# A decoder trunk on one core: some low parts of the weights are formed on GpSimd instead of VectorE

## The chip, the core and the metric

The kernel runs on one core of a Trainium2 chip. The core has a matrix engine, TensorE (PE), and three engines for elementwise work: VectorE (DVE), ScalarE (ACT) and GpSimd (POOL). SyncE (SP) issues most of the DMAs. Each engine works through its own queue strictly in order and waits on semaphores for results of the others. The metric is the device time of one execution in microseconds; the median of several runs is compared. A profile is one execution that the hardware profiler recorded.

## What is computed

Two layers of a decoder trunk, batch 1, 512 tokens, model width 1024, float32. Cut to what matters here:

```python
D_MODEL, SEQ, DEPTH, D_IN = 1024, 512, 2, 3488

def hybrid_layer(x, ...):
    h = rmsnorm(x, norm_g)
    p = h @ w_in
    (cq, ckv, kr, g_a, c_h, c_b, c_c, g_b, sg_u, sg_v, g_c, mq, mk, mv, g_d) = jnp.split(p, offs, axis=-1)
    o_a = causal attention on low-rank q and kv, with a rotary key
    o_b = c_b * short_conv(c_c * c_h, conv_w)
    o_c = spatial_gate(sg_u, sg_v, sg_ln_g, sg_ln_b, sg_w, sg_b)
    o_d = block-sparse attention on mq, mk, mv
    y = jnp.concatenate([o_a * silu(g_a), o_b * silu(g_b), o_c * silu(g_c), o_d * silu(g_d)], axis=-1)
    return y @ w_out

def reference(x, ...):
    for l in range(DEPTH):
        x = x + hybrid_layer(x, ...)
    return x
```

The lines for `o_a` and `o_d` are put in words here. The two large products are `h @ w_in` and `y @ w_out`.

## The kernel before

**Three matmuls for one.** A float32 operand is split in a high part in the form fp32r, and a low part, the rest, also fp32r. A product is three matmuls, high by high, high by low and low by high (`mm3`, L282). Weights and activations alike are split: the high part is a copy to fp32r, mostly on ACT, and the low part a subtraction, `lo = raw - hi`, on DVE.

**Weight units.** The weights come in units of at most 128 x 1024 numbers (`Unit`, named `ga0_0`, `b211_1` and so on: the name, and the layer behind the last underscore; in the profile's tile names the numbers are left out, so `wlo_b` is the low part of any of the units b110 to b221). All units stand in one list, `order`, in the order in which PE uses them, and `u.idx` is a unit's place there. `load_units` (L405) brings each by a DMA on SP's queue into a raw buffer; `split_units` (L439) makes it into `whi` and `wlo`, and does so in two halves: a half is 512 columns (416 for the units named c). A unit's raw buffer is free when both low halves are done, and the next load waits for it. There are two raw buffers and a few borrowed ones, and six pairs of `whi` and `wlo`.

**The planner.** The program is written out by a planner in Python, before anything runs. Each stretch of work is a generator; `Order` (L74) keeps a clock `o.now` that PE's matmuls advance by an assumed cost, and a clock for each other engine: `o.clk["A"]` for ACT, `"V"` for DVE, `"G"` for POOL, `"D"` for DMA. `Chain._emit` (L173) writes an instruction into its engine's queue when its operands are due by these clocks, and adds the assumed cost to the engine's clock. So the order in every queue is fixed by assumed costs, while the chip follows the semaphores. `at[0]` is the place of the unit that PE has reached, and a unit is "wanted" when it is less than `AHEAD` = 4 places on. `split_units` starts a half when ACT and DVE have nothing left by their clocks, or when the unit is wanted. `low_half` (L474) then holds the low half back while DVE is more than `VSLACK` = 300 ns behind and the unit is more than `URGENT` = 2 places ahead.

**What runs on POOL.** The rotary tables in the first 40 us; then a few powers that give reciprocal square roots (`pow_rstd`, L713: the tiles `ms`, `bmv`, `rs_q`, `rs_k`, `rs_mq`, `rs_mk`, `xss`), some fills (`kl0d`, `kl1d`), and accumulating DMAs (`t_sums`, L356). These last belong to the large products that are computed with seven products instead of eight: units named t1 to t4 (for `w_out`) and p1 to p4 (for a part of `w_in` in layer 1) are sums of blocks of the weights. They are built in DRAM by a copy on SP's queue and an adding DMA on POOL's queue, which waits for the copy; later copies wait for earlier sums.

**Stages that the prediction speaks of.** In each layer the products with activations come first, attention runs among them, and the last stage (`seven`, L1823) is `y @ w_out`: the products b11, t3, b21, t4, t2, t1 and b22. Each takes two units and 24 matmuls, 12 for each of two output tiles, so a unit is used up every 2.7 us there, twice as fast as elsewhere. A unit's two halves belong to two blocks of rows of the weights, and the second half is read three matmuls after the first or later; b211 is the second unit of b21, t41 that of t4. PE writes the results to PSUM tiles named oz, ox, oy and ot. DVE forms sums of activations there (`ys`, `u`), their low parts (`yTl`, `suml`) and the residual sums (`xr`).

Of the kernel before, what the change touches and what calls it, by code (L numbers as in the profile page):

```python
# [11 lines left out]
F32 = mybir.dt.float32  # L12
# [3 lines left out]
ALU = mybir.AluOpType  # L16
# [14 lines left out]

NRAW, NW, NT2 = 2, 6, 11
WSLACK = 0.0
AHEAD, URGENT, VSLACK = 4, 2, 300.0
NWARM, FILL, FILLEND = 6, 0.9, 15000.0
MIXT, MIXLAG, ROWT, COLT = 42000.0, 2000.0, 36000.0, 17500.0
KSPLIT, HMEAN = 6, 0.0
# [1 line left out]
LOPRIO = -5  # L39
# [119 lines left out]
def free_size(ap):  # L159
    n = 1  # L160
    for d in ap.shape[1:]:
        n *= d
    return n


class Chain:
# [24 lines left out]

    def pool(self, f, *a, **k):
        return self._emit("G", 290 + 2.0 * free_size(a[0]), f, a, k)

    def pow(self, f, *a, **k):
        return self._emit("G", 400 + 165 * free_size(a[0]), f, a, k)
# [24 lines left out]
def hybrid_trunk(ctx: ExitStack, tc: tile.TileContext, x, positions, norm_g, w_c, w_f, w_t, w_o, mla_q_norm_g,  # L221
# [3 lines left out]
    V, A, G, PE = nc.vector, nc.scalar, nc.gpsimd, nc.tensor  # L225
# [16 lines left out]
    o = Order()  # L242
# [196 lines left out]
    def split_units(i0, i1):  # L439
        for u in order[i0:i1]:  # L440
            ch = Chain(o)
            if u.name != "c0_0":
                yield from ch.wait(u.loaded)
            u.hi, u.lo = yield from u.slots.get(ch, u.name)
            n = u.a * u.b
            gain = {"uq": 2 * int(u.name[-1]), "ukv": 4 + int(u.name[-1])}.get(u.name[:-2])
            if gain is not None:
                yield from ch.wait(pc_ev)
            for i in range(2):
                if u.name == "c0_0":  # L450
                    yield from ch.wait(u.landed[i])
                while ch.t > o.now + SLACK:
                    yield ch.t - SLACK
                while not u.wanted and max(o.clk["A"], o.clk["V"]) > o.now + WSLACK:
                    yield o.now + 100.0
                sl = slice(i * n // 2, (i + 1) * n // 2)
                c2 = Chain(o, max(o.now, ch.t))
                hi, lo, raw = u.hi[:, sl], u.lo[:, sl], u.raw[:, sl]
                g = None
                if gain is not None:  # L460
                    c = gain + (i if u.a == 2 else 0)
                    g = pcol[:, c:c + 1]
                if o.clk["V"] + 600.0 < o.clk["A"] and u.idx > 3 or u.idx == 0 and i == 0:
                    if g is None:
                        yield from c2.dve_fast(V.tensor_copy, hi, raw)
                    else:
                        yield from c2.dve(V.tensor_scalar, hi, raw, g, None, op0=ALU.mult)
                else:
                    yield from c2.act(A.activation, hi, raw, AF.Copy, scale=1.0 if g is None else g)
                o.set(u.high[i], c2.t)  # L470
                o.spawn(low_half(u, i, c2, lo, raw, hi, g), None, LOPRIO if u.idx < 4 else 5)
                ch.t = max(ch.t, c2.t - LAT)

    def low_half(u, i, ch, lo, raw, hi, g):  # L474
        while o.clk["V"] > o.now + VSLACK and u.idx > at[0] + URGENT:
            yield o.now + 100.0
        ch.t = max(ch.t, o.now)
        if g is None:
            yield from ch.dve(V.tensor_tensor, lo, raw, hi.bitcast(F32), op=ALU.subtract)
        else:  # L480
            yield from ch.dve(V.scalar_tensor_tensor, lo, in0=raw, scalar=g, in1=hi.bitcast(F32),
                              op0=ALU.mult, op1=ALU.subtract)
        o.set(u.half[i], ch.t)
        if u.half[1 - i].t is not None:
            ch.t = max(ch.t, u.half[1 - i].t)
            u.raw_slots.put(ch)
            o.set(u.ready, ch.t)

# [9 lines left out]
    at = [0]  # L498
# [1507 lines left out]
    def start():  # L2006
# [32 lines left out]
        for u in order[:10]:  # L2039
            u.wanted = True  # L2040
        o.spawn(load_units(), None, 4)
        o.spawn(split_units(0, 4), None, LOPRIO)
        o.spawn(split_units(4, len(order)), None, 5)
        o.spawn(rope_tables(), 3700.0, 4)
        o.spawn(x_stats(), None, 5)
# [55 lines left out]
```

## Time and profile before

| what | value |
|---|---|
| median of 3 runs | 489.66 us (489.42 to 490.87) |
| the profiled execution's own time | 489.51 us |
| its span, first to last instruction | 487.8 us |
| granted TensorE clock, mean | 0.999 |
| TensorE busy | 480.9 us, 2432 matmuls |
| VectorE busy | 402.3 us, 897 instructions |
| ScalarE busy | 329.7 us, 912 instructions |
| GpSimd busy | 104.0 us, 172 instructions |
| DMA | 92.89 MB, mean 190 GB/s |

How to read the lines in this document. In a timeline or a chain a line begins with the start and the length in microseconds, then the engine, the line of the kernel, the operation, and the tiles `out<-in` with their shapes; a bracket at the end tells how long the engine sat idle before it and what ended that. Most instructions have L178, the line of the planner that emits them, and matmuls L208; so tiles tell them apart. In a group, `x32 | 20.8, 682` means 32 instructions, 20.8 us busy, 682 ns of one on average. In the waits, `A <- B: total, times, longest` means that engine and tile A waited for B. Instructions of an engine overlap a little, so a duration can be longer than the distance between two starts. The ends of matmuls are modelled; their starts are recorded.

### The profile page before, as it was taken

Reading aid. Unit: us, or ns where it says so; the run is one execution under the profiler, and the core shown is the slowest. Engines: PE = TensorE matmul, PEld = TensorE weight load, DVE = VectorE, ACT = ScalarE, POOL = GpSimd, SP = SyncE. Lnnn points to the kernel's source line nnn. Section 1 sums busy time; section 2 is a strip of 40 time slices with the busy share of each in tenths; the row PEclk is TensorE's granted clock in tenths of the full one; section 3 lists DMA queues with packets and bytes.
Section 4 is the critical chain, followed back from the end, with each engine's and each line's share of the span. In section 5 each row is a group of like instructions: output and inputs, shape, how many; then the busy total and the mean of one; then the engine's idle time right before and its main releaser. Section 6 shows DMA issues by size and latency. Waiting matters only on the chain.

```text
span 487.8 us, 7534 instructions
## 1 busy us (share of the span) xinstructions
PE 480.9 (99%) x2432; PEld 408.4 (84%) x2432; DVE 402.3 (82%) x897; ACT 329.7 (68%) x912; POOL 104.0 (21%) x172
## 2 busy tenths in 40 slices
PE   8999999999999999999999999999999999999997
PEld 8987888888878888888899988888888888888786
DVE  3687788769788897789898688979788998997993
ACT  6887857766447885447577788768675687666740
POOL 7864150710321020000031013520402200000000
PEclk9999999999999999999999999999999999999999
DMA  8433536997599688875663286786832744427762
GB/s 285 173 105 114 172 116 230 235 197 152 178 315 283 171 208 209 289 264 202 206 237 141 80 285 241 176 243 169 209 132 87 151 141 140 173 66 264 275 215 88
DMA packets 41904, 92.89 MB, mean 190 GB/s; under 512 B 7158, under 2 KB 23048, under 8 KB 41480
## 3 DMA queue, kind: packets, MB, share of 16 engines
q1 hardware_dynamic: 29168, 79.82, 47.1%
q0 software_dynamic: 12672, 12.58, 16.7%
q8 instruction: 19, 0.31, 0.3%
q14 instruction: 21, 0.17, 0.1%
q10 hardware_dynamic: 24, 0.01, 0.0%
HBM read 84.53 MB, written 33.03 MB: 241 GB/s over the span
## 4 chain that ended last, share of the span: by engine, by line
PE 96%; DVE 2%; ACT 0%; issue 0%; DVEq 0%; ACTq 0%
PE cq L208 8%; PE oy L208 6%; PE kv L208 6%; PE gd L208 5%; PE gb L208 5%; PE cb L208 5%; PE ch L208 5%; PE su L208 5%; PE gc L208 5%; PE cc L208 5%; PE ga L208 4%; PE sq L208 4%; PE oz L208 4%; PE py L208 3%; PE ox L208 3%; PE sa L208 3%
## 5 line engine op out<-in xcount | busy, mean ns | idle before, releaser
L178 ACT ACTIVATE pd<-pd,mnd 128x384 f32<-128x384 f32 (+3 forms) x48 | 25.4, 550 | 3.1 <-DVE mnd L178 2.8
L178 ACT ACTIVATE pha<-pTa 128x512 fp32r<-128x512 f32 (+3 forms) x32 | 13.9, 435 | 19.4 <-PE pTa L208 19.1
L178 ACT ACTIVATE pa<-pa,mna 128x384 f32<-128x384 f32 (+3 forms) x46 | 24.3, 550 | 2.4 <-DVE mna L178 2.3
L178 ACT ACTIVATE phd<-pTd 128x512 fp32r<-128x512 f32 (+3 forms) x32 | 13.9, 437 | 14.5 <-PE pTd L208 14.2
L372 POOL DMA_DIRECT2D t<-in_w_o_dram x16 | 17.2, 1323 | 22.3 <-DMA t<-t 22.3
L178 DVE TENSOR_TENSOR wlo_p<-raw_p,whi_p 128x512 fp32r<-128x512 f32 x28 | 19.1, 698 | 3.1 <-ACT whi_p L178 2.9
L178 DVE TENSOR_TENSOR pla<-pTa,pha 128x512 fp32r<-128x512 f32 (+3 forms) x32 | 15.3, 486 | 7.2 <-ACT pha L178 7.1
L208 PE MATMUL cq<-whi_c,hTh 128*128 128x416 f32 x64 | 20.5, 366 | 0.3 <-ACT hTh L178 0.3
L178 DVE TENSOR_TENSOR wlo_t<-raw_t,whi_t 128x512 fp32r<-128x512 f32 x32 | 20.8, 682 | 0.0
L208 PE MATMUL cq<-wlo_c,hTh 128*128 128x416 f32 x64 | 20.0, 359 | 0.0
L208 PE MATMUL cq<-whi_c,hTl 128*128 128x416 f32 x64 | 19.9, 356 | 0.0
L178 DVE CUSTOM_DVE_ANT_0 pa<-sa,maskb,rs_q 128x512 f32<-128x512 f32 (+3 forms) x32 | 16.5, 545 | 3.9 <-PE pTa L208 2.0
L178 ACT ACTIVATE whi_t<-raw_t 128x512 fp32r<-128x512 f32 x30 | 17.4, 618 | 1.6 <-DMA raw_t<-t 1.6
L178 DVE CUSTOM_DVE_ANT_0 pd<-sd,maskb,rs_mq 128x512 f32<-128x512 f32 (+3 forms) x32 | 16.9, 545 | 1.4 <-PE pTd L208 0.8
L178 POOL TENSOR_TENSOR rs_mk<-rs_mk,nhalf 128x16 f32<-128x16 f32 x2 | 6.2, 3083 | 51.1 <-DVE rs_mk L178 51.1
L178 DVE TENSOR_TENSOR pld<-pTd,phd 128x512 fp32r<-128x512 f32 (+3 forms) x32 | 15.2, 485 | 2.3 <-ACT phd L178 2.2
L178 POOL TENSOR_SCALAR xss<-xss 128x1 f32<-128x1 f32 x4 | 2.7, 670 | 66.1 <-ACT jk L178 61.8
L178 ACT ACTIVATE whi_b<-raw_b 128x512 fp32r<-128x512 f32 x23 | 14.0, 622 | 3.5 <-DMA raw_b<-in_w_o_dram 3.5
L178 ACT ACTIVATE whi_p<-raw_p 128x512 fp32r<-128x512 f32 x22 | 13.2, 624 | 4.4 <-DMA raw_p<-in_w_t_dram 4.4
L178 DVE TENSOR_TENSOR wlo_b<-raw_b,whi_b 128x512 fp32r<-128x512 f32 x24 | 16.0, 684 | 0.2
L208 PE MATMUL pTa<-ident,pa 128*128 128x128 f32 x80 | 14.0, 273 | 0.0
L208 PE MATMUL pTd<-ident,pd 128*128 128x128 f32 x80 | 13.9, 272 | 0.0
(470 smaller groups left out, 1853.3 us busy)
## 6 DMA issues: line engine op xcount, KB each, us to landing
t<-in_w_o_dram POOLq DMA_DIRECT2D x16, 512.0 KB, 8.1
raw_t<-t SPq DMA_DIRECT2D x16, 512.0 KB, 3.2
raw_b<-in_w_o_dram SPq DMA_DIRECT2D x12, 512.0 KB, 4.6
t<-in_w_o_dram SPq DMA_DIRECT2D x8, 512.0 KB, 4.4
p<-in_w_t_dram POOLq DMA_DIRECT2D x8, 512.0 KB, 13.1
t<-t SPq DMA_DIRECT2D x8, 512.0 KB, 6.8
raw_p<-p SPq DMA_DIRECT2D x8, 512.0 KB
ys<-ysc SPq DMA_DIRECT2D x14, 256.0 KB, 4.2
```

Source lines behind the costliest of these rows:

```text
L178: f(*a, **k)
L208: f(*a, **k)
L372: nc.gpsimd.dma_start(src(l, n, j), src(l, y, j), accum_op=ALU.add, max_dma_last_dim=1024)
```

## The change

The low part of a unit can now go to POOL. `split_units` forms the high part of a unit whole, in one instruction, when the unit is more than `WHOLE` = 2 places ahead of PE, has no gain and the clock is past `WHOLET` = 50,000 ns; otherwise in halves as before. `low_half` becomes `low_part`, which takes one half or both. While the unit is more than `URGENT` places ahead it asks, every 100 ns of the planner's clock: if POOL's queue is empty by its clock (and the unit has no gain and is more than `PLEAD` = 2 places ahead, past `WHOLET`), it emits the subtraction on POOL in pieces of `PCOLS` = 256 columns; if DVE is less than `VSLACK` behind, it goes to DVE in one instruction, 512 or 1024 columns wide; otherwise it asks again. The assumed cost of a piece on POOL is 200 + 1.65 ns a column.

```diff
-AHEAD, URGENT, VSLACK = 4, 2, 300.0
+AHEAD, URGENT, VSLACK, WHOLE, WHOLET = 4, 2, 300.0, 2, 50000.0
+PLEAD, GSLACK, PCOLS = 2, 0.0, 256
...
+    def pool2(self, f, *a, **k):
+        return self._emit("G", 200 + 1.65 * free_size(a[0]), f, a, k)
...
-            for i in range(2):
+            parts = [0, 1]
+            while parts:
+                i = parts[0]
...
-                sl = slice(i * n // 2, (i + 1) * n // 2)
+                ids = parts if i == 0 and gain is None and u.idx > at[0] + WHOLE and o.now > WHOLET else parts[:1]
+                parts = parts[len(ids):]
+                sl = slice(i * n // 2, (i + len(ids)) * n // 2)
...
-                o.set(u.high[i], c2.t)
-                o.spawn(low_half(u, i, c2, lo, raw, hi, g), None, LOPRIO if u.idx < 4 else 5)
+                for j in ids:
+                    o.set(u.high[j], c2.t)
+                o.spawn(low_part(u, ids, c2, lo, raw, hi, g), None, LOPRIO if u.idx < 4 else 5)
                 ch.t = max(ch.t, c2.t - LAT)
 
-    def low_half(u, i, ch, lo, raw, hi, g):
-        while o.clk["V"] > o.now + VSLACK and u.idx > at[0] + URGENT:
+    def low_part(u, ids, ch, lo, raw, hi, g):
+        while u.idx > at[0] + URGENT:
+            if g is None and u.idx > at[0] + PLEAD and o.clk["G"] <= o.now + GSLACK and o.now > WHOLET:
+                ch.t = max(ch.t, o.now)
+                for c in range(0, free_size(lo), PCOLS):
+                    z = slice(c, min(c + PCOLS, free_size(lo)))
+                    yield from ch.pool2(G.tensor_tensor, lo[:, z], raw[:, z], hi[:, z].bitcast(F32), op=ALU.subtract)
+                for j in ids:
+                    o.set(u.half[j], ch.t)
+                if None not in (u.half[0].t, u.half[1].t):
+                    ch.t = max(u.half[0].t, u.half[1].t)
+                    u.raw_slots.put(ch)
+                    o.set(u.ready, ch.t)
+                return
+            if o.clk["V"] <= o.now + VSLACK:
+                break
             yield o.now + 100.0
...
-        o.set(u.half[i], ch.t)
-        if u.half[1 - i].t is not None:
-            ch.t = max(ch.t, u.half[1 - i].t)
+        for j in ids:
+            o.set(u.half[j], ch.t)
+        if None not in (u.half[0].t, u.half[1].t):
+            ch.t = max(u.half[0].t, u.half[1].t)
             u.raw_slots.put(ch)
             o.set(u.ready, ch.t)
```

Because the planner's clocks change, it also writes the other instructions of the queues in another order from there on: PE has the same matmuls, with attention placed differently among the products.

## The prediction

> **What bounds the kernel now.** I read the page's totals first, then the waits of TensorE, then the chain of work that ended last.
>
> ```profile
> span 487.8 us, 7534 instructions
> PE 480.9 (99%) x2432; PEld 408.4 (84%) x2432; DVE 402.3 (82%) x897; ACT 329.7 (68%) x912; POOL 104.0 (21%) x172
> PE 96%; DVE 2%; ACT 0%; issue 0%; DVEq 0%; ACTq 0%
> ```
> ```profile
> PE sd L208 <- ACT mk0d L178: 0.8, 1, 0.8
> ...
> PE gd L208 <- DVE zz L178: 0.3, 1, 0.3
> ...
> PE oz L208 <- DVE wlo_b L178: 0.3, 1, 0.3
> ```
> ```profile
> 216.10 5.44 PE ox L208 x24
> ```
>
> TensorE (PE) is the bound. A busy row alone would not prove it, since its ends are modelled, but the chain does: 24 matmuls of 512 columns in 5.44 us are 0.227 us each, all along the kernel, and 96% of the chain is PE. The view of PE's waits shows these three after the first 50 us, where the change begins to act (its three others are in the head):
>
> ```profile
> 141.70 0.39 PE L208 MATMUL gd<-hTh,wlo_gd 128*128 128x512 f32 x1
> 142.91 0.50 PE L208 MATMUL sd<-mk0d,mq0d 128*128 128x512 f32 x1 [0.82 <-ACT mk0d L178]
> ...
> 457.36 0.61 PE L208 MATMUL oz<-whi_b,yD 128*128 128x512 f32 x2
> 458.24 0.50 PE L208 MATMUL oz<-wlo_b,yD 128*128 128x512 f32 x1 [0.27 <-DVE wlo_b L178]
> ```
>
> By the distance of the starts, the first cost 1.21 - 0.23 = 0.98 us and the third 0.88 - 0.45 = 0.43; for the second I take its wait, 0.3. Together 1.7 us: the most that freeing VectorE (DVE) and ScalarE (ACT) can give, because the change leaves the number and widths of the matmuls alone. A low part that comes late has no such limit.
>
> **The change part by part.** In the built program's order, 158 low parts of 512 columns and 16 of 416 on DVE become 23 of 1024, 15 of 512, 2 of 832 and 8 of 416, and GpSimd (POOL) gets 200 pieces of 256 columns and 2 of 64. On ACT, 143 high parts of 512 become 59 of 1024 and 12 of 512; on DVE 15 become 12 of 1024 and 4 of 512.
>
> ```profile
> L178 DVE TENSOR_TENSOR wlo_t<-raw_t,whi_t 128x512 fp32r<-128x512 f32 x32 | 20.8, 682 | 0.0
> L178 ACT ACTIVATE whi_t<-raw_t 128x512 fp32r<-128x512 f32 x30 | 17.4, 618 | 1.6 <-DMA raw_t<-t 1.6
> L178 POOL TENSOR_TENSOR rope_scratch<-ones,rope_scratch 128x128 f32<-128x128 f32 x1 | 0.4, 403 | 0.1
> L178 POOL TENSOR_TENSOR rd<-ident,xv 128x512 f32<-128x512 f32 x1 | 1.0, 1042 | 0.1
> 456.56 0.42 DVE L178 TENSOR_TENSOR ys<-ys 128x256 f32<-128x256 f32 x1
> 456.90 0.69 DVE L178 TENSOR_TENSOR suml<-ys,sumh 128x512 fp32r<-128x512 f32 x1
> 457.50 0.69 DVE L178 TENSOR_TENSOR wlo_b<-raw_b,whi_b 128x512 fp32r<-128x512 f32 x1
> ```
>
> Packed, a DVE low part of 512 columns takes 0.60 us from start to start (456.90 to 457.50) and 256 columns 0.34, so 256 columns more cost 0.26 and 1024 about 1.13. DVE's low parts go from 158 x 0.60 + 16 x 0.50 = 103 us to 23 x 1.13 + 15 x 0.60 + 2 x 0.93 + 8 x 0.50 = 41 us (832 and 416 columns in proportion): 62 us of work fewer. ACT saves the fixed part of 143 - 71 = 72 instructions, and each whole part holds its queue for up to 2 x 0.62 = 1.24 us. None of this is on the path by itself; it can only shorten the three waits.
>
> POOL shows no such piece. From 128 to 512 columns its two-input operations take 639 ns more, that is 1.66 ns a column, so 256 columns take 403 + 128 x 1.66 = 616 ns alone: 200 x 0.62 + 2 x 0.29 = 125 us, and POOL goes from 104 to 229 us of 488. Its output form (fp32r) is in no POOL row. This is hidden while each piece ends before its matmul. The bound from above comes from these rows:
>
> ```profile
> 38.91 1.04 POOL L178 TENSOR_TENSOR rd<-ident,xv 128x512 f32<-128x512 f32 x1
> ...
> 287.90 1.01 POOL L178 COPY K<-krt 128x512 f32<-128x512 f32 x1 [6.12 <-DVE krt L178]
> ```
> ```profile
> 39.24 1.26 DVE L178 TENSOR_TENSOR wlo_sq<-raw_sq,whi_sq 128x512 fp32r<-128x512 f32 x1
> ...
> 287.75 1.70 DVE L178 TENSOR_TENSOR wlo_p<-raw_p,whi_p 128x512 fp32r<-128x512 f32 x2
> ```
>
> A low part on DVE beside a reading POOL operation took 1.26 us instead of 0.68: it ended 0.55 us after POOL did, as if it had started only then. The pair at 287.75 took 1.70 instead of 0.60 + 0.69 = 1.29. So the two do not run together, and a piece costs 0.62 us alone and up to 0.62 + 0.60 = 1.22 where DVE runs such operations back to back. I take 0.9, the middle, since DVE operations that read PSUM stand between them. DVE in turn pays up to 0.62 us per piece that it meets.
>
> The Trainium skill ("SBUF — State Buffer", section Who interferes with whom) states this as a rule that speaks against the change: a DVE instruction with two SBUF inputs and a GpSimd instruction that reads SBUF exclude each other for the whole instruction. The rows agree. By that rule alone every piece that meets such DVE work gives back more (0.62 us) than the 0.30 us of DVE time that it takes over; that is the slower rival below.
>
> Where it counts is the last stage of each layer (products b11 to b22), where DVE works back to back:
>
> ```profile
> 460.91 0.69 DVE L178 TENSOR_TENSOR wlo_t<-raw_t,whi_t 128x512 fp32r<-128x512 f32 x1
> 461.51 0.69 DVE L178 TENSOR_TENSOR suml<-ys,sumh 128x512 fp32r<-128x512 f32 x1
> ...
> 463.13 0.39 PE L208 MATMUL ox<-wlo_t,yD 128*128 128x512 f32 x1
> ```
>
> - Unit t41 of layer 1. Before, its halves stand 22 matmuls ahead of the first reader; the first ended at 461.60, 1.5 us before 463.13. After, one part of 1024 stands 19 ahead: 0.68 us later, and 0.53 longer. Ahead of it DVE loses four halves (2.4 us) to eight pieces on POOL, which block it by 0 to 5.0 us; I take 3.0, so 0.6 net (-2.4 to +2.6). End: 461.60 + 0.68 + 0.53 + 0.6 = 463.4. The reader, no longer held 0.43 at 457, is due at 462.7: a new wait of 0.7 us (0 to 2.7).
> - Unit b211 of layer 1, whose last half caused the wait at 458.24. Its four pieces stand 25, 22, 19 and 13 matmuls ahead instead of halves at 19 and 10. The last is read by the second half's matmuls, three later than the unit's first, so from the first piece there are 28 x 0.227 = 6.4 us; four pieces take 3.6 at 0.9 and 4.9 at 1.22. The wait goes: -0.4 (0 if DVE's other work makes one in its place).
> - Unit b211 of layer 0: 22, 19, 16 and 10 ahead, with two pieces of t40 between them. From the first piece to the reader of the last there are 25 x 0.227 = 5.7 us; six pieces take 3.7 to 7.3, at 0.9 5.4. +0.2 (0 to 1.6).
> - Other short distances: c2 of layer 1 (last piece 11 ahead), p211 (13), kv3 (12), ga1 of layer 1 (5). Behind each I count the second-half matmuls still to come. ga1's last piece is queued behind a power on POOL:
>
> ```profile
> L178 POOL TENSOR_TENSOR rs_q<-rs_q,nhalf 128x16 f32<-128x16 f32 x2 | 6.6, 3294 | 6.5 <-DVE rs_q L178 6.5
> ```
>
> It is read 18 matmuls after the unit's first low part, so 23 x 0.227 = 5.2 us after its place, which the rest of the 3.29 us just leaves. For all four +0.5 (0 to 2).
> - The wait of gd on DVE: gone, with 62 us less on DVE, -0.3 (0 to -0.3). The wait of sd on mk0d stays: its chain begins with a 2.9 us power on POOL, now behind pieces of gd0: 0 (-0.98 to +0.7).
> - The accumulating DMAs:
>
> ```profile
> 90.88 4.60 POOL L372 DMA_DIRECT2D t<-in_w_o_dram  x4
> 129.90 2.93 POOL L178 TENSOR_TENSOR rs_mk<-rs_mk,nhalf 128x16 f32<-128x16 f32 x1 [30.18 <-DVE rs_mk L178]
> 171.31 1.01 POOL L372 DMA_DIRECT2D t<-in_w_o_dram  x1 [9.93 <-DMA t<-t]
> ```
>
> ```profile
> 136.06 0.47 SPq L367 DMA_DIRECT2D p<-p  x1
> ```
>
> The issues that went out in one batch from 90.88 us, eight in all, now stand between the pieces of ch0, cc0 and gd0, which wait for their high parts, the last of them behind the power of 129.90. So they go out up to some 30 us later, and SP's copies that need them wait in SP's queue with raw weights behind them. But the copies of p, at 136.06 and after, need only the fifth and sixth issue, ahead of gd0's pieces. A piece behind an issue can wait up to 9.9 us, and stands 60 to 100 matmuls (14 to 22 us) ahead there. 0 (0 to +3).
>
> Sum: 0.7 - 0.4 + 0.2 + 0.5 - 0.3 = +0.7 us. The profiled execution's own time is 489.51 us (487.8 of span and 1.7 around it), 0.15 below the median of the three runs, 489.66; 489.51 + 0.7 = **490.2 us**.
>
> **The rivals.**
> - Faster: DVE at (402 - 62) / 488 = 70% instead of 82% keeps up everywhere, the three waits go and no new one comes. For it: 62 us off DVE, and most pieces stand farther ahead than the halves did. Against it: the blocking rows. 489.5 - 1.7 = 487.8 us.
> - Slower, by the exclusion of POOL and DVE: in both last stages pieces take the full 1.22 us and DVE is held 0.62 by each of the eight around t40. It decides from about 0.95 us a piece, where b211 of layer 0 begins to be late. t41 2.7, b211 1.6, the short distances 1.0 or more, the old waits kept: 489.5 + 5.3 at the full price, 2.5 at half; I put it at 492.5 us.
> - The DMAs moved later hold SP's queue, and raw weights behind them come late: +3, 492.5 us. Against it: that stretch's weights are split 14 to 22 us ahead of their matmuls.
> - That POOL is rarely found idle, so that little moves, is excluded by the order: 202 pieces are there.
>
> **How the numbers follow.** Less than 0.3% (1.5 us) can't be told from no change here. The forecast's own range is 489.0 to 491.6: chance 0.40, three quarters of it within 0.3%, a quarter slower. Faster rival 0.27 (four in five beyond 0.3%), exclusion 0.26, DMAs 0.07, both slower by over 0.3% nearly always. So faster 0.23, same 0.37, slower 0.40. The range that should hold 8 in 10 goes from just below the faster rival, 487.6, to the exclusion's price at half and a little more, 493.2.
>
> **What would show it.** PE's matmul count and 5.44 us per 24 stay. Right: DVE about 345 us busy plus blocking, POOL over 200, POOL pieces between 0.62 and 1.2 us, the longer ones beside DVE low parts; no wait of oz on wlo_b at the end of layer 1; a short wait of ox on a DVE wlo_t near 463. Wrong: PE waits on POOL of more than 2 us in all, pieces over 1.3 us, SP waiting for t or p copies around 130 to 180 us, or no PE wait at all after 50 us.

## The result and the profile after

| | before | after |
|---|---|---|
| time, median of the runs of one session | 490.26 us (489.42 to 493.88) | 513.87 us (513.41 to 514.46) |
| ratio, 95% interval | 1 | 1.0484 (1.0453 to 1.0515) |
| span of the profiled execution | 487.8 us | 511.9 us |

The change made the kernel 4.8% slower, 23.6 us. First the page's totals, the row of granted TensorE clock (40 slices, tenths of full speed) and the shares of the chain of waits, of the kernel after:

```profile
span 511.9 us, 7568 instructions
PE 490.9 (96%) x2432; PEld 412.8 (81%) x2432; DVE 382.9 (75%) x770; ACT 313.7 (61%) x814; POOL 285.3 (56%) x374
PEclk9999999999999999997999999898999999999998
PE 58%; DVE 13%; DMA 9%; POOL 8%; issue 6%; ACT 5%; SPq 1%; POOLq 0%; DVEq 0%; ACTq 0%
```

TensorE executes the same 2432 matmuls, but its share of the chain has fallen from 96% to 58%. DVE, DMA and POOL have taken the rest. No engine has become the bound by its busy time: DVE is at 75%, less than before. The clock, a row of nines in the kernel before, has four slices at 0.7 or 0.8.

The six longest rows of TensorE's waits after the first 50 us (total us, times, longest), of after:

```profile
PE py L212 <- DVE x L179: 2.7, 1, 2.7
PE oy L212 <- DVE xr L179: 2.3, 1, 2.3
PE ox L212 <- DVE wlo_t L179: 2.1, 1, 2.1
PE ox L212 <- ACT whi_t L179: 1.7, 1, 1.7
PE py L212 <- DVE th_ga L179: 1.4, 1, 1.4
PE oz L212 <- POOL wlo_b L179: 1.2, 1, 1.2
```

The three waits of before (sd on mk0d, gd on zz, the last oz on wlo_b) are gone, as the change promised. In their place stand longer ones, and only one of them is on a piece that GpSimd formed. The others are on DVE's ordinary results (x, xr, th_ga) and on parts of weights that ACT and DVE formed late (whi_t, wlo_t).

To see where the time went I summed, for both kernels, by how much each matmul starts later after the one before it than its width needs (0.227 us for 512 columns). The excess of after over before is 8.4 us in the last stage of layer 0, 3.2 in that of layer 1, 7.9 in the products p of layer 1, 5.7 in the attention's matmuls and -1.1 elsewhere: 24.1 us, the same as the difference of the spans.

Three of these places show how it comes about. First, GpSimd and DVE shut each other out (timeline of after, one engine after the other: start us, us, engine, operation, idle time before it and what ended it):

```profile
346.02 1.22 DVE L179 TENSOR_TENSOR wlo_p<-raw_p,whi_p 128x1024 fp32r<-128x1024 f32 x1
347.15 1.21 DVE L179 TENSOR_TENSOR yTl<-a,yTh 128x512 fp32r<-128x512 f32 x1
...
349.15 0.68 DVE L179 TENSOR_TENSOR x<-py,x 128x512 f32<-128x512 f32 x1
...
346.09 4.93 POOL L179 TENSOR_TENSOR wlo_cc<-raw_cc,whi_cc 128x256 fp32r<-128x256 f32 x4
...
349.88 0.80 PE L212 MATMUL py<-whi_p,yTh 128*128 128x512 f32 x1 [2.74 <-DVE x L179]
350.48 0.63 PE L212 MATMUL py<-wlo_p,yTh 128*128 128x512 f32 x1
```

A yTl of 512 columns, with both inputs in SBUF, takes 1.21 us here; x, as wide but with one input from PSUM, takes 0.68 beside the same pieces. The four pieces take 4.93 us together, 1.23 each. The operation x, which stands behind it in DVE's queue, has nothing to do with the pieces, and TensorE waits 2.74 us for it. The exclusion is not the whole of this wait. The chain of waits goes back from x to bmv, a reciprocal square root on POOL: its input was ready at 338.16, but POOL came to it at 343.96, after a wait for another load, the issue of a DMA and two pieces of wlo_p. So a piece also delays what stands behind it in POOL's own queue. After the pause the next matmuls start 0.43 us apart instead of 0.23: TensorE's granted clock is halved (the rows are in the last section).

Second, the raw buffer, in the last stage of layer 0. These are single rows from the timelines of POOL, SP (its DMA queue), DVE, ACT and PE, after:

```profile
214.85 3.82 POOL L179 TENSOR_TENSOR wlo_t<-raw_t,whi_t 128x256 fp32r<-128x256 f32 x4 [12.91 <-ACT whi_t L179]
218.69 0.80 SPq L299 DMA_DIRECT2D raw_t<-t  x2
219.54 5.03 SPq L299 DMA_DIRECT2D ys<-ysc  x7
226.62 0.42 DVE L179 TENSOR_TENSOR ys<-ys,ys 128x256 f32<-128x256 f32 x1 [5.17 <-DMA ys<-ysc]
227.96 0.63 ACT L179 ACTIVATE sumh<-ys 128x512 fp32r<-128x512 f32 x1 [4.82 <-DVE ys L179]
231.50 1.99 ACT L179 ACTIVATE whi_t<-raw_t 128x1024 fp32r<-128x1024 f32 x2
232.59 0.50 PE L212 MATMUL ox<-whi_t,yD 128*128 128x512 f32 x1 [1.66 <-ACT whi_t L179]
233.94 1.21 DVE L179 TENSOR_TENSOR wlo_t<-raw_t,whi_t 128x1024 fp32r<-128x1024 f32 x1
235.21 0.80 PE L212 MATMUL ox<-wlo_t,yD 128*128 128x512 f32 x1 [2.12 <-DVE wlo_t L179]
```

A load of raw_t leaves at 218.69, 0.02 us after the last piece of a unit has ended (214.85 + 3.82 = 218.67): it was waiting for that unit's raw buffer. Behind it in SP's queue stand the loads of ys, parts of the activations that have nothing to do with the pieces; they go out from 219.54 on. DVE sits idle for 5.17 us until they land, and ACT for 4.82 us until DVE has formed a sum from them. All that stands behind these operations comes late: the high part whi_t, for which TensorE waits 1.66 us, and the low part wlo_t, for which it waits 2.12 us. The raw data of that whi_t had landed at 224.01; it is the queue that is late, not this load.

Third, both together, in the chain of waits near the end of after (start us, us, what):

```profile
483.34 5.59 POOL wlo_t L179 x3
...
488.95 0.34 SPq L299
...
489.41 5.12 DMA raw_b<-in_w_o_dram
...
494.64 1.07 ACT whi_b L179
...
497.48 0.69 DVE xr L179
...
498.21 4.84 PE oy L212 x13
```

The pieces of a unit hold a raw buffer until 488.94, the load of raw_b leaves then, lands 5.1 us later, and DVE, which works in order, stands at the low part of that unit while the sum xr, for which TensorE waits 2.27 us, stands behind it.

That loads wait for raw buffers was to be read in the trace of before. Its view of SP's waits:

```profile
SPq L295 <- DVE wlo_ch L178: 36.4, 4, 23.2
SPq L295 <- DVE wlo_b L178: 33.1, 8, 7.0
SPq L295 <- DVE wlo_cc L178: 32.4, 4, 11.0
```

With seven more such rows (wlo_gb, wlo_gc, wlo_kv, wlo_su, wlo_p, wlo_cb, wlo_t) SP spends 244 of 488 us waiting for the low part that frees the buffer. So whatever makes a low part end later can make the load behind it leave later. These waits do not slow the kernel before, since its loads still come in time.

### The profile page after: what moved, and what is told of

It is laid out like the page before. It is cut to its first block, busy times and chain, and to the rows that moved or that the text cites. A ratio compares the mean times of both kernels' runs of the same rounds, so it can differ in the third digit from the quotient of the medians.

```text
span 511.9 us, 7568 instructions
## 1 busy us (share of the span) xinstructions
PE 490.9 (96%) x2432; PEld 412.8 (81%) x2432; DVE 382.9 (75%) x770; ACT 313.7 (61%) x814; POOL 285.3 (56%) x374
## 4 chain that ended last, share of the span: by engine, by line
PE 58%; DVE 13%; DMA 9%; POOL 8%; issue 6%; ACT 5%; SPq 1%; POOLq 0%; DVEq 0%; ACTq 0%
PE cq L212 7%; PE oy L212 5%; PE kv L212 4%; PE gd L212 4%; PE gb L212 3%; PE cb L212 3%; PE cc L212 3%; PE gc L212 3%; PE sa L212 2%; POOL wlo_t L179 2%; PE sd L212 2%; DMA raw_t<-t 2%; PE py L212 2%; DMA dq_b<-in_moba_q_g_dram 2%; PE pTa L212 2%
## 5 line engine op out<-in xcount | busy, mean ns | idle before, releaser
L179 POOL TENSOR_TENSOR wlo_t<-raw_t,whi_t 128x256 fp32r<-128x256 f32 x32 | 36.5, 1171 | 24.6 <-ACT whi_t L179 24.6
L179 POOL TENSOR_TENSOR wlo_b<-raw_b,whi_b 128x256 fp32r<-128x256 f32 x32 | 27.6, 892 | 16.0 <-PE od L212 8.3
L179 ACT ACTIVATE pa<-pa,mna 128x128 f32<-128x128 f32 (+3 forms) x53 | 27.5, 547 | 4.3 <-DVE mna L179 3.8
L179 ACT ACTIVATE pd<-pd,mnd 128x128 f32<-128x128 f32 (+3 forms) x49 | 25.6, 544 | 5.2 <-DVE mnd L179 4.8
L179 POOL TENSOR_TENSOR wlo_ch<-raw_ch,whi_ch 128x256 fp32r<-128x256 f32 x16 | 15.0, 952 | 20.7 <-DVE whi_ch L179 11.4
L179 POOL TENSOR_TENSOR wlo_cb<-raw_cb,whi_cb 128x256 fp32r<-128x256 f32 x16 | 12.8, 823 | 22.3 <-ACT whi_cb L179 22.3
L179 POOL TENSOR_TENSOR wlo_gb<-raw_gb,whi_gb 128x256 fp32r<-128x256 f32 x16 | 15.2, 979 | 16.8 <-issue 13.9
L179 ACT ACTIVATE pha<-pTa 128x512 fp32r<-128x512 f32 (+3 forms) x32 | 13.9, 436 | 16.1 <-PE pTa L212 15.8
L179 POOL TENSOR_TENSOR wlo_p<-raw_p,whi_p 128x256 fp32r<-128x256 f32 x20 | 18.0, 973 | 8.6 <-ACT whi_p L179 5.3
L179 ACT ACTIVATE whi_t<-raw_t 128x1024 fp32r<-128x1024 f32 x16 | 16.4, 1048 | 10.2 <-DMA raw_t<-t 10.2
L179 POOL TENSOR_TENSOR wlo_su<-raw_su,whi_su 128x256 fp32r<-128x256 f32 x12 | 10.3, 940 | 15.7 <-DVE whi_su L179 10.6
```

The lines of the kernel that those rows point to most:

```text
L179: f(*a, **k)
```

## The experiments

Theory X: a reading GpSimd operation and DVE's operations with two SBUF inputs exclude each other; that lengthens DVE's own chain. Theory H: the pieces hold the raw buffers longer, so loads leave later. Rivals: W, the whole parts come too late; P, the planner's order is what costs. "Before" ran beside each group of kernels (490.2 to 490.7 us).

### Parts of the change alone

**Whole parts without pieces, and pieces without whole parts.**

```diff
-PLEAD, GSLACK, PCOLS = 2, 0.0, 256
+PLEAD, GSLACK, PCOLS = 10 ** 6, 0.0, 256          # e1_whole
-AHEAD, URGENT, VSLACK, WHOLE, WHOLET = 4, 2, 300.0, 2, 50000.0
+AHEAD, URGENT, VSLACK, WHOLE, WHOLET = 4, 2, 300.0, 10 ** 6, 50000.0   # e2_pieces
```

> The whole high and low parts alone: no piece goes to GpSimd, 69 low parts of 1024 columns stay on DVE. Theory X (POOL's pieces and DVE's two-input operations hold each other up) and theory H (pieces on POOL hold the raw buffers longer, so loads go out later): about the time of before, 489 to 492 us, granted clock 0.99 or more. Rival W (parts of 1024 columns come too late for the first matmuls that read them): 500 us or more, with the PE waits on whi_t, wlo_t and wlo_b of the changed kernel still there.

> Pieces on GpSimd alone: 200 of 256 columns as in the changed kernel, but every high part in halves and the low halves left on DVE in halves. X and H: most of the loss stays, 505 to 514 us. W: back near before, under 495 us.

Measured: whole parts alone 493.9 us, ratio 1.0069 (1.0044 to 1.0094); pieces alone 506.8 us, 1.0337 (1.0299 to 1.0375). The whole parts are not free, 3.7 us where X and H gave at most 2, but they are no rival for the loss. Most of it comes with the pieces. With pieces alone TensorE's longest wait is on a piece itself (5.0 us on a wlo_t), which does not happen in the changed kernel.

**The same order, the pieces on VectorE.**

```diff
-yield from ch.pool2(G.tensor_tensor, lo[:, z], ...
+yield from ch.pool2(V.tensor_tensor, lo[:, z], ...
```

> The changed kernel's order with the 202 pieces issued on VectorE instead of GpSimd (the planner still books them on GpSimd). DVE's work is then 345 + 200 x 0.34 = 413 us, against 402 before, and nothing is excluded. X: 490 to 496 us, POOL 104 us busy, DVE operations at their lengths of before. Rival P (the changed order of the instructions on ACT, DVE and SP is what costs, whoever executes the pieces): 505 us or more. H lies between: the raw buffers are still freed after four pieces, but four of 0.34 instead of four of 1.0 us, 491 to 498.

Measured: 503.5 us, 1.0269 (1.0225 to 1.0312). This lies below P's figure and above those of X and H. DVE was busy 411.7 us, as foreseen, and without a reserve its queue comes late with everything: no wait of TensorE is longer than 1.5 us, but there are many. By itself this run can't clear P, and none of the theories gave its time; the next group explains it.

**Extra GpSimd work in the kernel before.**

```diff
+            if u.idx > at[0] + 1 and u.idx % 3 and o.now > 50000.0:
+                for c in range(0, free_size(lo), 256):
+                    z = slice(c, min(c + 256, free_size(lo)))
+                    G.tensor_tensor(junk[:, :z.stop - c], lo[:, z].bitcast(F32), lo[:, z].bitcast(F32), op=ALU.subtract)
```

> The kernel before, whose order and buffers are untouched, plus 201 two-input GpSimd operations of 256 columns that read low parts already written and put their result into a scratch tile that nothing reads. Extra work, no result depends on it. X: DVE's two-input operations stretch as in the changed kernel (yTl from 0.73 to about 1.1 us on average), DVE busy rises by 40 us or more, and the time by 5 to 25 us. H and P: no buffer is held longer and no order changes, so within 1.5 us of before.

Measured: 537.7 us, 1.0963 (1.0907 to 1.1019), twice the loss of the change. The run shows more than it was made for: the scratch tile junk is also written by ACT for its sums of squares, so ACT waits for POOL (34.6 us in 16 waits, the longest 4.8), and POOL, in order, waits for DVE's low parts. DVE is busy 26.6 us longer (428.9 against 402.3) and yTl takes 0.89 us: the direction of X, but less than the 40 us and 1.1 us that it gave. The time proves nothing about X alone.

### Reading and holding, one at a time

The next kernels keep the changed kernel's order, instruction for instruction, and replace the 202 pieces. What a piece reads and whether it touches the raw tile can then be set separately. A piece that does not touch the raw tile leaves its buffer free as soon as the high part is formed, earlier than in any of the kernels that compute the low part.

```diff
-yield from ch.pool2(G.tensor_tensor, lo[:, z], raw[:, z], hi[:, z].bitcast(F32), op=ALU.subtract)
+yield from ch.pool2(lambda d: (G.memset(d, 0.0), G.memset(d, 0.0)), lo[:, z].bitcast(F32))             # e6_memset
+yield from ch.pool2(G.tensor_tensor, lo[:, z], hi[:, z].bitcast(F32), hi[:, z].bitcast(F32), op=ALU.subtract)  # e7_read_hi
+yield from ch.pool2(lambda d: (G.memset(d, 0.0), G.memset(raw[:, z], 0.0)), lo[:, z].bitcast(F32))     # e10_hold
+yield from ch.pool2(lambda d: (G.memset(d, 0.0), G.memset(d, 0.0), G.memset(raw[:, z], 0.0)), ...      # e11_hold_long
+yield from ch.pool2(G.tensor_copy, lo[:, z], hi[:, z])                                                  # e12_copy_hi
```

> The changed kernel in its own order, but each piece on GpSimd is two memsets of the same 256 columns (about 0.62 us together, from 522 ns for 512 columns) instead of the subtraction: POOL is as busy as it would be alone, reads nothing from SBUF and does not hold the raw buffer. The low parts of those units are zero. X: DVE's operations go back to their lengths of before and the loss goes, 489 to 495 us. Rival P (the order and the queues that the planner chose cost, whoever does the work and whatever it reads): 505 us or more. H: the raw buffers are free early as well, so this run alone does not tell H from X.

> As the run with memsets, but each piece is one two-input operation that reads the high part twice and not the raw tile: same reads of SBUF and same length as the real piece, while the raw buffer is free after its high part. The low parts of those units are zero. X: pieces of about 1 us and stretched DVE operations as in the changed kernel, 505 to 514 us. H: as with the memsets, 489 to 496 us. The difference between this and the changed kernel is what holding the raw buffers costs.

> The changed kernel's order; each piece is a memset of its 256 columns of the low part and a memset of the same 256 columns of the raw tile (0.62 us together). It reads nothing, but it waits for the high part, as the real piece does, and holds the raw buffer until the last piece. The low parts of those units are zero. The step from reading the high part alone (501.1) to the changed kernel (513.9) was 12.8 us. H (the held buffers cost by themselves): 495 us or more, SP waiting on POOL again. X alone (holding costs only because DVE's work beside it makes the pieces long): 487 to 491 us.

> As the run before it with one memset more per piece, 0.93 us, about the 0.97 us that a piece took in the changed kernel: pieces of the real length, the raw buffers held as long, and no read. H: 498 to 504 us, the held buffers at their real length without any effect on DVE. X alone: 487 to 492 us.

> The changed kernel's order; each piece is a GpSimd copy of the high part, so one input from SBUF instead of two, the raw buffer not held. The low parts of those units hold the high part instead of the rest. If any reading GpSimd operation shuts DVE's two-input operations out: as with two reads of the high part, 498 to 502 us, yTl near 1.1 us. If it takes two inputs on POOL: as with memsets, 487 to 490 us, yTl 0.68 us.

| pieces | reads | holds raw | time | ratio (95%) | DVE busy | yTl 512 |
|---|---|---|---|---|---|---|
| two memsets | no | no | 487.2 us | 0.9929 (0.9902 to 0.9956) | 349.4 us | 0.68 us |
| copy of the high part | one input | no | 489.5 us | 0.9967 (0.9941 to 0.9993) | 356.6 us | 0.90 us |
| high part twice | two inputs | no | 501.1 us | 1.0199 (1.0153 to 1.0245) | 378.5 us | 1.13 us |
| memsets, raw too | no | yes | 499.6 us | 1.0177 (1.0105 to 1.0248) | 354.6 us | 0.68 us |
| the same, 0.93 us | no | yes | 498.6 us | 1.0179 (1.0154 to 1.0203) | 349.1 us | 0.68 us |
| the change | two inputs | yes | 513.9 us | 1.0484 (1.0453 to 1.0515) | 382.9 us | 1.09 us |

The rows behind the last two columns, the groups by line of the kernel with memsets, of that with two reads, of the changed one (out and in, number, then total us and mean ns):

```profile
L179 DVE TENSOR_TENSOR yTl<-a,yTh 128x512 fp32r<-128x512 f32 x8 | 5.2, 682 | 0.5 <-ACT yTh L179 0.5
```
```profile
L179 DVE TENSOR_TENSOR yTl<-a,yTh 128x512 fp32r<-128x512 f32 x8 | 8.8, 1131 | 0.0
```
```profile
L179 DVE TENSOR_TENSOR yTl<-a,yTh 128x512 fp32r<-128x512 f32 x8 | 8.5, 1085 | 0.0
```

What follows:

- The order costs nothing by itself: with the pieces' work on POOL neither reading nor holding, the kernel is 3.4 us faster than before, and its chain is TensorE throughout:

```profile
PE 99%; DVE 0%; issue 0%; DVEq 0%
```

  P falls in the form that it had, that the order costs whoever does the work and whatever it reads. No kernel here has this order and real low parts without losing time.
- Reading costs 501.1 - 487.2 = 13.9 us. The 501.1 us lie between the range of X and that of H, so neither has the whole loss. The Trainium skill ("SBUF — State Buffer", section Who interferes with whom) says that a GpSimd instruction that only writes does not contend with a DVE instruction with two SBUF inputs, and one that reads does. The memset runs (yTl 0.68 us) and the reading runs (0.90 and 1.13) agree.
- Holding costs 499.6 - 487.2 = 12.4 us, and no more when the pieces take 0.93 us. DVE is hardly lengthened: it is busy 5 us longer in the first of the two runs (its operations with one input beside memsets) and not at all in the second. X alone, which gave 487 to 492 us, falls; both runs lie in the range that H gave. But the length of a piece, which H had as the cause, is not what costs. The traces show what does: count, for each of the 95 loads of weights, the matmuls that TensorE had started when the load was issued, and compare with the same load in the kernel with two memsets. On average the loads leave 3 matmuls later with the copies and 3 with two reads, but 11 and 14 in the two runs that hold, 16 in the changed kernel, and 17 in the run with the pieces on VectorE. So the 503.5 us of that run fit the late loads as well, and it is not POOL's queue in particular: in this order a low part that reads the raw tile frees it late on either engine.
- A piece that reads the high part or writes the raw tile also has to wait, in POOL's queue, for the high part, which two memsets of the low part do not. That wait is in both steps; the copies have it too, and they cost 2.3 us in all, so it can't be more.
- 13.9 + 12.4 = 26.3 us, and the step from memsets to the change is 513.9 - 487.2 = 26.7: the two together make up the loss. This is a little too neat. The run that holds is known only to some 3 us (495.0 to 501.5), and a piece of the changed kernel is longer than one that reads the high part twice: 0.73 us against 0.61 where it meets little (10th percentile of the 202).
- My either-or for the copy was wrong. One-input copies do lengthen DVE's work, but a copy takes only 0.40 us alone, so it holds less, and 7.2 us more of DVE time cost 2.3 us where 29.1 us more cost 13.9.

How a held buffer turns into a stall, in the run that holds and does not read (timelines of SP, ACT and PE):

```profile
319.96 0.81 SPq L299 DMA_DIRECT2D raw_p<-in_w_t_dram  x2
...
328.96 1.06 ACT L179 ACTIVATE whi_p<-raw_p 128x1024 fp32r<-128x1024 f32 x1 [5.66 <-DMA raw_p<-in_w_t_dram]
329.93 0.67 ACT L179 ACTIVATE hi1a<-t1a,pcol 96x512 fp32r<-96x512 f32 x1
...
330.64 0.80 PE L212 MATMUL sa<-hi1a,hi0a 96*128 96x512 f32 x1 [2.86 <-ACT hi1a L179]
```

The two loads leave at 319.96, when a low part of DVE frees the buffer; in the kernel with two memsets they leave at 307.75 and 308.96. ACT stands 5.66 us before a load that has not landed; behind it in the queue is hi1a, a part of the attention's keys that has nothing to do with that weight, and TensorE waits 2.86 us for that. The late weight itself is not what it waits for.

### The plan's prices, and where the pieces are

```diff
-        return self._emit("G", 200 + 1.65 * free_size(a[0]), f, a, k)
+        return self._emit("G", 430 + 2.2 * free_size(a[0]), f, a, k)         # e8_priced, e9_priced_v
+                    o.clk["V"] = max(o.clk["V"], o.now) + 400.0              # e9_priced_v, after each piece
-            if g is None and u.idx > at[0] + PLEAD and ...
+            if g is None and u.name[:-3] not in ZPROD + SPROD and u.idx > at[0] + PLEAD and ...   # e13_feat
```

> The changed kernel with the planner told what a piece took in its trace: 430 + 2.2 ns a column, 0.99 us instead of 0.62 for 256 columns; 181 pieces are left. P: most of the loss goes, 497 us or less. X and H: the pieces still meet DVE's work and still hold the raw buffers, 500 to 512 us.

> As the run before it, and for each piece the planner also books 0.4 us on VectorE, about what DVE loses to a piece that it meets; 196 pieces are left. P in the form that the plan does not know of the lost DVE time: 495 us or less. X and H: 500 to 512 us, since a plan that knows of the lost time cannot give it back.

> The changed kernel with pieces on GpSimd for feature, token and c units alone (108 of 256 columns and 2 of 64); the units of the products p and b/t have their low parts on DVE, whole where their high parts are. If the loss sits in the product stages, as most of the long PE waits in the trace do: near the run with whole parts alone, 492 to 497 us. If it goes with the number of pieces, half of the step from that run to the changed kernel: 502 to 505 us.

Measured: 511.4 us (1.0408, 1.0366 to 1.0449), 507.4 us (1.0354, 1.0311 to 1.0398) and 503.5 us (1.0272, 1.0235 to 1.0308). A plan that knows the real prices gives back 2.5 and 6.5 of 23.6 us, within what X and H gave. And the loss goes with the number of pieces: with 108 instead of 200 about half of the step from the whole parts (493.9) to the change (513.9) is left, though no piece is in a product stage any more. There the excess of the p products is gone, while the last stage of layer 0 costs 8.9 us (8.4 in the changed kernel), by waits on ACT's whi_b and DVE's wlo_b. The chain of waits shows where these come from (start us, us, what; single rows):

```profile
186.84 2.50 POOL wlo_su L179 x3
189.35 0.33 SPq L299
201.60 8.51 DMA raw_t<-t
221.01 6.41 DMA ys<-ysc
231.01 2.07 PE oz L212 x4
```

The pieces of su, a unit that is split before that stage, hold a raw buffer until 189.34. SP stands there; then it issues the loads behind, at 201.60 one of raw_t, and the loads of ys after it go out late as well. In the changed kernel the same pieces end at 188.67 and that load of raw_t leaves at 200.40; in the kernel with two memsets SP goes on at 181.7 and the load leaves at 192.0, while TensorE reaches the stage only 2.5 us sooner than in the changed kernel. So a held buffer is paid for in a later stage, which has no pieces.

### More raw buffers, and a version that might beat both

```diff
-NRAW, NW, NT2 = 2, 6, 11
+NRAW, NW, NT2 = 4, 5, 11      # before: e14; changed: e15; with the pieces of e10: e17; of e6: e18; of e7: e19
```
```diff
+                if g is None and o.now > 50000.0 and u.idx > at[0] + 2 and o.clk["G"] <= o.now:     # e16_hi_on_pool, on the kernel before
+                    yield from c2.pool(G.tensor_copy, hi, raw)
```

> The kernel before with four raw buffers instead of two and five pairs of high and low tiles instead of six (the same SBUF). It is the base for the two runs beside it. Nothing waits for raw buffers on its path, so within 3 us of before, 488 to 493 us, by every theory.

> The changed kernel with the same buffers; 213 pieces of 256 columns. If the held raw buffer costs because there are only two: about 14 us over the kernel before with these buffers, the exclusion alone, so 502 to 507 us. If it costs for another reason: 22 us or more over it, 510 us or more.

> The run that holds the raw buffer and reads nothing (a memset of the low part and one of the raw tile per piece), with four raw buffers. Shortage of raw buffers: the 12 us go, 486 to 491 us. Another reason: 497 us or more. The low parts of those units are zero.

> Four raw buffers, five pairs; each piece is two memsets of the low part: nothing read, nothing held. The low parts of those units are zero. If the raw buffers were what the hold lacked, the run that holds (494.5) is within 3 us of this one: 491 to 494 us here. If the hold costs as much as with two buffers: 482 to 485 us here, which is below what TensorE's matmuls leave room for, so then about 487 us and a step of 7 us.

> Four raw buffers, five pairs; each piece reads the high part twice, raw buffer not held. The low parts of those units are zero. If the exclusion grew and the hold is gone: 515 to 521 us, next to the changed kernel with these buffers (520.7). If the exclusion stays at its 14 us and the hold brings the rest: 503 to 508 us.

> The kernel before with 68 high parts of 512 columns and 2 of 416 copied on GpSimd (one input) instead of ACT and DVE, for units more than two ahead, when the planner has GpSimd free. [...] If the chain load, high part, low part has slack of about 0.5 us (a copy of 512 columns takes 0.81 us on POOL, 0.62 on ACT): 488 to 491 us. If the raw buffers are what counts, they come free later by POOL's queue: 493 to 500 us.

| | two raw buffers | four raw buffers, five pairs |
|---|---|---|
| before | 490.3 us | 491.2 us |
| neither reads nor holds | 487.2 | 493.0 |
| holds | 499.6 | 494.5 |
| reads | 501.1 | 501.0 |
| reads and holds | 513.9 | 520.7 |

The run that holds, 494.5 us, lies between the two ranges that were given for it; against its own base of 493.0 us, with the same buffers, holding alone costs 1.5 us instead of 12.4. So it was the shortage of raw buffers, as far as holding alone goes. Reading alone costs 8.0, its 501.0 us below both ranges. But both together cost 27.7, and here the two do not add up: the 502 to 507 us that I expected of the changed kernel are missed by far. TensorE's largest waits in that run are on DVE's results and on POOL's pieces (6.1 us in all on pa, 4.8 on wlo_t), and its loads again leave late, by 12 matmuls on average against 7 in the run that only holds, counted as above from the run that does neither. Five pairs of high and low tiles instead of six, 213 pieces instead of 200, and longer pieces than in the run that reads the high part twice are all in it, and I could not separate them. So this corner stays open.

High parts copied on GpSimd, in the kernel before: 499.0 us, 1.0171 (1.0138 to 1.0204). The time lies in the range given for late raw buffers, but no run separates that from the other effects of the copies. The copies of a 512-column part take 0.66 to 1.27 us on average, by the unit, and DVE is busy 5.6 us longer. No version with real work on POOL was faster than the kernel before.

## Why the prediction was wrong

- **Which step failed.** "This is hidden while each piece ends before its matmul." In the changed kernel the pieces do end in time, all but one: TensorE waits 1.2 us in all for a piece. I looked for the cost where a low part meets its own reader, and priced lateness in four or five places. The cost came from two things that a piece does on its way: it blocks DVE, which delays whatever stands next in DVE's queue, and it keeps a raw buffer, which delays the next load. The first I had as a rival and sized it from the two last stages alone; the second was in no term.
- **The raw buffers.** 12.4 us by the run that holds and does not read. The rows of SP's waits, quoted above, were there before the change; the prediction did not use them. My rival in which raw weights come late had a different cause, DMA issues that hold SP's queue. That cause did not happen: no row of SP's waits in the changed kernel is on a copy of t or p, and the accumulating DMAs stand in the same places in the run with memsets, which is faster than before. Nothing here speaks against its zero.
- **The exclusion.** The sizes were near. I took 0.9 us a piece; it was 0.97 (196.3 us for 202), and POOL's 285.3 us is what 104 + 200 x 0.9 gives. The piece alone, put at 0.62 from f32 rows of other widths, took 0.73. DVE paid 382.9 - 349.4 = 33.5 us, 0.17 a piece, far from the 0.62 that I gave as the most. But what 33.5 us of lost DVE time cost, 492.5 us as a rival, was too little: alone it is 501.1.
- **The three waits.** They went, sd on mk0d as well, which I had left in. With pieces that neither read nor hold the kernel reaches 487.2 us; the faster rival's 487.8 was the right figure for a change without side effects.
- **The short distances.** t41 of layer 1: +0.7 predicted, no wait. b211 of layer 1: the wait went, as predicted. b211 of layer 0: +0.2 predicted with a bound of 1.6, measured 1.2. c2, p211, kv3, ga1: +0.5 predicted, no wait. These terms were roughly right and did not decide the time. The waits of 1.7 and 2.1 us on a unit of t4 in layer 0, shown above, were in no term.
- **The clock.** Not in the sum at all. After the first 50 us 25 matmuls of the changed kernel start about twice as far apart as usual; together they take 4.9 us too much, a fifth of the loss. In the trace of before there is none. It is a consequence of the pauses, and how much of it the time would lose without it is not shown: three other executions had a mean clock of 0.987 to 0.993 instead of 0.983, and were no faster (513.4 to 514.5 us).
- **The whole parts.** Taken as able to gain only; alone they lose 3.7 us.
- **The signs.** Of the signs of being wrong that the prediction named, one came: 20 of the 202 pieces took more than 1.3 us, the longest 2.7.

## What to carry to other kernels

Moving work to an idle engine is not judged by whether the result is there in time: list what the work keeps while it runs (a buffer whose release gates a load, the other engine's operations that it shuts out) and who stands behind that in each in-order queue. Look at the DMA queue's own waits before moving the last reader of a buffer: where they are long and end with the operation that frees it, a later release moves the loads, and all that stands behind them in that queue, even if no compute engine waits for DMA yet. Long waits alone do not show that buffers are short: with four of them the kernel before took 491.2 us, not less than with two (490.3). To find which of several side effects costs, keep the order of the changed kernel and replace the moved operation by ones that write only, read only, or hold only.

## What the runs showed of the hardware

- A GpSimd operation with one SBUF input lengthens DVE's two-input operations too (yTl 0.90 us against 0.68), a memset does not (0.68). A memset does hold up DVE operations with one input: a CAST of 1024 columns took 1.13 us beside three memsets (at 454.17 us of the run that holds) and 0.69 beside none.
- Two SBUF inputs from two tiles cost GpSimd 0.73 us for 256 columns, the same tile twice 0.61, one input 0.40, and a memset 0.31 (each the 10th percentile of 200 or more).
- TensorE's granted clock falls to half after a pause. In the kernel after, from the view of windows (the stretch, its us; busy us and instructions of PE, PEld, DVE, ACT, POOL; then the clock, DMA's share and GB/s):

```profile
346.00:349.30 3.30, 1.15 (x6) 0.61 (x4) 3.30 (x6) 1.23 (x3) 3.30 (x4) 1.00 0.43 161
349.40:352.70 3.30, 2.81 (x7) 2.26 (x8) 3.30 (x6) 3.30 (x8) 2.28 (x3) 0.50 0.18 25
```

  The matmuls of 512 columns then start 0.427 us apart for 2 to 4 us. The Trainium skill ("TensorE: Matmul & The Clock Gate", Part 1: The HAM clock gate) gives 426.7 ns for the halved clock, which agrees, and an idle window of about 3.4 us as its condition. Here gaps of 3.1 us (346.76 to 349.88) and 2.7 us (495.55 to 498.21) between two starts were enough, the second with a delay of 1.7 us before the first slow matmul. In the trace's record of the clock the half clock begins at 233.26, 325.42, 349.32 and 499.50 us, which are whole multiples of 3.41 us apart, and lasts 3.41 or 6.83 us each time.
